# Seven up-projection pairs in seven products instead of five, and DRAM block sums handed out at other places: one core of a Trainium2

## The chip, the cores and the metric

The kernel runs on one core of one Trainium2 chip. The metric is the device time of one execution in microseconds: median 826.57 us of three runs before the change (824.71 to 828.17). Five engines work side by side: TensorE (PE; its weight loads, PEld, overlap its matmuls), VectorE (DVE), ScalarE (ACT), GpSimd (POOL) and SyncE (SP), which only issues DMAs. Sixteen DMA engines move data for the queues of SP, ACT and POOL.

## The reference, cut to what matters

One layer of an encoder, float32, 512 tokens of width 1024, 256 memory tokens:

```python
h = rmsnorm(x, pre_mix_g)
aq, ak, av, hq, hf_fwd, hf_bwd, hi, hg = split_columns(h @ w_in)
att = axial_gqa_attention(rope(rmsnorm(aq)), rope(rmsnorm(ak)), av)   # 8 heads of 64, 2 key heads
rec = hgrn2_group(hq, hf_fwd, hf_bwd, hi, hg)                         # 4 heads of 128, both directions
x = x + rmsnorm(concat(att, rec) @ w_out, post_mix_g)
x = x + rmsnorm(cross_attention(rmsnorm(x, pre_x_g), rmsnorm(mem), w_xq, w_xkv, w_xo), post_x_g)
u = rmsnorm(x, pre_ffn_g) @ w_up                                      # 1024 -> 2 x 2816
acc = conv_b + sum(shift(u, j - 1) * conv_w[j] for j in range(3))     # over positions
gate, val = split(acc)
x = x + rmsnorm((silu(gate) * val) @ w_down, post_ffn_g)              # 2816 -> 1024
```

## The kernel before, in words

**Every product in three matmuls.** TensorE multiplies in float32r. Each operand is split into a rounded high part and a low part (the rest), and a product is the sum of high x high, high x low and low x high (`mm3`, L242, its three matmuls on L243 to L245). The high part is a cast on ScalarE, the low part a subtraction on VectorE (`split`, L117, its two operations on L118 and L119).

**Weights come in units.** All projections but the last read weights in units of 128 x 1024, numbered in the order of their use: `plan` lists them, 0 to 65 (`N_MIX`) for the token mixing and the cross-attention, then the up projection, then 42 of the down projection. `take` and `unit` (L231 to L240) are called where TensorE wants the next unit; each call also hands out work for units `AHEAD` = 3 further on: `issue` (L198) loads the unit on SP's queue (`load_w`, L167), casts its high part and makes its low part. High and low parts have four buffers each (`wp`, L95), raw units two, and two more in the up projection (`raw_room`, L154). From unit 70 on loads also run ahead of the casts, `LOAD_AHEAD` = 5 units before their use (L228). For units 7 to 30 (`NEG_SCALAR`) the low part is not VectorE's: ScalarE writes minus the high part (L214) and a DMA on POOL's queue adds the raw weight from DRAM onto it (L217); for units 31 to 41 (`NEG_POOL`) POOL does the negation (L216).

**Order on the engines.** The framework sets the semaphores and lays the instructions of each engine in order, near the program's but not always in it; `tc.issue_after(ins)` holds an instruction behind another. Each engine works in order, and a wait at its head stops all behind it.

**Stages.** Input projection and four recurrent heads (`hgrn_core`), each a chain of small matmuls (L607) and VectorE products (L633); self-attention, woven with the keys and values of the memory; output projection and residual; queries and cross-attention; output projection and residual, where `turn_in` (L278) transposes the normalized rows into `hT`; up projection with convolution (`conv`, L1036); down projection.

The keys are transposed by `turn_k` (L711) into PSUM banks with the tag "b", two of them, which the memory's key projection uses as well. `rope_tables` (L668) scales the rope tables on ScalarE. The last `turn_in` also lets ScalarE copy the unsplit transposed rows to `fulls` (`keep`, L288 and L289).

**The up projection.** 22 pairs of a gate block and a value block of 128 columns. A whole pair takes two units and 2 x 8 products of 512 columns, three matmuls each. The pairs in `UP_S` = (5, 8, 11, 14, 17) are done by Strassen's scheme in Winograd's form (`strassen_pair`, L1094): seven products of 512 x 128 blocks with half of the tokens (256 columns) instead of eight. They take four units: "diag" and "side" are loaded, "sums" and "last" are sums of blocks that VectorE makes (`add_blocks`, L184). Differences of halves of the tokens come from `fulls` (`sum_of_h`, L1078, in pairs 2 and 3).

**The down projection.** The same scheme over the whole product: seven products (`PRODUCTS`) over the 22 activation blocks, in three groups (`GROUPS`). Four of the seven right sides are sums of blocks of `w_down`, built in DRAM by DMAs in six pieces each: a seed copy of one block and an accumulating DMA of another (`new_sums`, L989), called after pairs 2, 5, 8, 11, 14 and 17. The first seed of a kind goes to ACT's queue, seeds from an earlier sum to POOL's (L994), and the accumulating ones to POOL's (L998). The left sides are differences of activations (`group_sides`, L1001, called at pairs 18 and 19 and after the last) and are split by `left_side` (L1010), three ahead (`LAY_AHEAD`). For the (product, group) in `NEG_GROUP` their low part is a negation on POOL (L1023) and an accumulating DMA that reads the side itself (L1024). For product 3 the side is overwritten in place (L1014).

## Time and profile before

| | |
|---|---|
| time of the profiled execution | 825.72 us |
| its span, first to last instruction | 823.8 us |
| median of the three runs | 826.57 us |
| granted clock of TensorE | 0.999 |
| TensorE matmul / VectorE / ScalarE / GpSimd busy | 808.1 / 568.5 / 473.0 / 132.3 us |
| low parts by DMA on POOL's queue | 35 of 512 KB |
| DMAs for sums in DRAM (seeds and accumulating ones) | 48, of them 36 on POOL's queue and 12 on ACT's |
| moved by DMA | 135.66 MB, mean 165 GB/s |

How to read the rows: a row of the timeline has start (us), duration (us), engine, line, operation, output <- inputs, partitions x elements, how often in a row; in brackets stands how long the engine had stood idle before it, and what ended that. A row of groups has the count after the x, then busy us and mean ns. A row of waits has the engine and line that waited, what for, and us in total, times, longest. Matmuls overlap, so their step is read from starts, not from durations. A line in a helper (L118, L119, L243 to L245) stands for many uses; the tile's name tells them apart: `ps_b` is a PSUM bank of tag b, `wh` and `wl` are high and low parts of weights, `raw` and `tmp` unsplit weights, `sum_t` a sum in DRAM, `big` one of sixteen large buffers.

### The profile page before, as it was taken

Reading aid. Unit: us, or ns where it says so; the run is one execution under the profiler, and the core shown is the slowest. Engines: PE = TensorE matmul, PEld = TensorE weight load, DVE = VectorE, ACT = ScalarE, POOL = GpSimd, SP = SyncE. Lnnn points to the kernel's source line nnn. Section 1 sums busy time; section 2 is a strip of 40 time slices with the busy share of each in tenths; the row PEclk is TensorE's granted clock in tenths of the full one; section 3 lists DMA queues with packets and bytes.
Section 4 is the critical chain, followed back from the end, with each engine's and each line's share of the span. In section 5 each row is a group of like instructions: output and inputs, shape, how many; then the busy total and the mean of one; then the engine's idle time right before and its main releaser. Section 6 shows DMA issues by size and latency. Waiting matters only on the chain.

```text
span 823.8 us, 11495 instructions
## 1 busy us (share of the span) xinstructions
PE 808.1 (98%) x4354; PEld 690.6 (84%) x4354; DVE 568.5 (69%) x849; ACT 473.0 (57%) x785; POOL 132.3 (16%) x194
## 2 busy tenths in 40 slices
PE   9999999999999999999999999999999999999996
PEld 7878888889898887888888898889889888878884
DVE  5347486569886875855453769787687796868865
ACT  6666756369788874645543665444344453556651
POOL 0110211044233101300001300111110102100302
PEclk9999999999999999999999999999999999999999
DMA  9696753657668533252212145787898885368842
GB/s 316 186 283 134 173 112 95 129 140 162 160 155 191 116 136 120 77 179 78 88 43 101 37 163 153 205 232 202 224 279 217 232 250 146 103 200 295 249 124 102
DMA packets 39671, 135.66 MB, mean 165 GB/s; under 512 B 5120, under 2 KB 6656, under 8 KB 39424
## 3 DMA queue, kind: packets, MB, share of 16 engines
q1 hardware_dynamic: 25632, 86.03, 30.0%
q0 software_dynamic: 10960, 40.38, 25.5%
q10 hardware_dynamic: 3024, 8.53, 2.9%
q8 instruction: 34, 0.56, 0.3%
q14 instruction: 21, 0.17, 0.1%
HBM read 130.72 MB, written 25.17 MB: 189 GB/s over the span
## 4 chain that ended last, share of the span: by engine, by line
PE 84%; DMA 4%; DVE 4%; issue 3%; ACT 2%; POOL 2%; SPq 0%; POOLq 0%; DVEq 0%; ACTq 0%
PE ps_b L243 9%; PE ps_b L244 9%; PE ps_b L245 9%; PE ps_s L244 6%; PE ps_s L245 6%; PE ps_s L243 6%; PE ps_o L243 5%; PE ps_o L245 5%; PE ps_o L244 5%; PE ps_c L245 4%; PE ps_c L244 4%; PE ps_c L243 4%; PE ps_c L607 3%; PE ps_o L851 2%; PE ps_s L830 2%
## 5 line engine op out<-in xcount | busy, mean ns | idle before, releaser
L119 DVE TENSOR_TENSOR wl<-raw,wh 128x1024 fp32r<-128x1024 f32 (+1 forms) x75 | 90.7, 1212 | 64.1 <-ACT wh L118 63.8
L118 ACT CAST wh<-raw 128x1024 fp32r<-128x1024 f32 (+1 forms) x75 | 76.8, 1027 | 83.0 <-PE ps_b L244 25.7
L243 PE MATMUL ps_b<-big,wh 128*128 128x512 f32 (+1 forms) x340 | 122.4, 360 | 0.7 <-DVE big L119 0.7
L245 PE MATMUL ps_b<-big,wl 128*128 128x512 f32 (+1 forms) x340 | 120.5, 355 | 0.0
L244 PE MATMUL ps_b<-big,wh 128*128 128x512 f32 (+1 forms) x340 | 120.5, 354 | 0.0
L243 PEld LDWEIGHTS ps_b<-big,wh 128*128 128x128 f32 x340 | 64.3, 189 | 9.2 <-DVE big L119 0.9
L244 PEld LDWEIGHTS ps_b<-big,wh 128*128 128x128 f32 x340 | 64.3, 189 | 8.6
L245 PEld LDWEIGHTS ps_b<-big,wl 128*128 128x128 f32 x340 | 64.2, 189 | 8.7
L633 DVE TENSOR_TENSOR big<-big 128x512 f32<-128x512 f32 x64 | 48.4, 761 | 16.4 <-PE ps_c L607 10.1
L244 PE MATMUL ps_s<-wl,big 128*128 128x512 f32 (+1 forms) x140 | 53.4, 381 | 2.6 <-DVE wl L119 1.7
L243 PE MATMUL ps_s<-wh,big 128*128 128x512 f32 (+1 forms) x140 | 53.5, 384 | 0.4 <-DVE big L119 0.4
L245 PE MATMUL ps_s<-wh,big 128*128 128x512 f32 (+1 forms) x140 | 53.1, 379 | 0.0
L212 ACT CAST wh<-raw 128x1024 fp32r<-128x1024 f32 x35 | 36.8, 1052 | 26.7 <-PE ps_b L244 12.9
L217 POOL DMA_DIRECT2D wl<-in_w_dram x35 | 30.9, 883 | 120.1 <-ACT wl L214 105.1
L119 DVE TENSOR_TENSOR big<-ps_o,big 128x512 fp32r<-128x512 f32 x54 | 37.0, 688 | 14.1 <-ACT big L118 12.2
L998 POOL DMA_DIRECT2D sum_t<-in_wd_dram x24 | 19.7, 833 | 143.7 <-DMA sum_t<-in_wd_dram 86.8
L118 ACT CAST big<-ps_o 128x512 fp32r<-128x512 f32 x54 | 31.6, 589 | 17.2 <-PE ps_o L953 7.5
L243 PE MATMUL ps_o<-wh,big 128*128 128x512 f32 (+1 forms) x102 | 39.3, 386 | 0.0
L244 PE MATMUL ps_o<-wl,big 128*128 128x512 f32 (+1 forms) x102 | 38.2, 375 | 0.0
L245 PE MATMUL ps_o<-wh,big 128*128 128x512 f32 (+1 forms) x102 | 38.2, 374 | 0.0
L244 PE MATMUL ps_c<-big,wh 128*128 128x256 f32 (+1 forms) x112 | 37.6, 336 | 0.0
L243 PE MATMUL ps_c<-big,wh 128*128 128x256 f32 (+1 forms) x112 | 37.6, 336 | 0.0
(311 smaller groups left out, 2171.0 us busy)
## 6 DMA issues: line engine op xcount, KB each, us to landing
raw<-in_w_dram SPq DMA_DIRECT2D x85, 512.0 KB, 3.3
wl<-in_w_dram POOLq DMA_DIRECT2D x35, 512.0 KB, 5.4
sum_t<-in_wd_dram POOLq DMA_DIRECT2D x20, 512.0 KB, 8.1
tmp<-in_w_dram SPq DMA_DIRECT2D x14, 512.0 KB, 6.0
sum_t<-in_wd_dram ACTq DMA_DIRECT2D x10, 512.0 KB, 6.2
sum_t<-sum_t POOLq DMA_DIRECT2D x10, 512.0 KB, 5.2
big<-sum_t SPq DMA_DIRECT2D x10, 512.0 KB, 4.9
raw<-sum_t SPq DMA_DIRECT2D x10, 512.0 KB, 4.5
```

The source lines that it names most:

```text
L118: nc.scalar.copy(hi, src)
L119: (eng or nc.vector).tensor_sub(lo, src, hi.bitcast(F32))
L212: nc.scalar.copy(wh, raw)
L217: nc.gpsimd.dma_start(wl, io["w"][i], accum_op=ALU.add)
L243: nc.tensor.matmul(o, a[0], b[0], start=start, stop=False, skip_group_check=again)
L244: nc.tensor.matmul(o, a[0], b[1], start=False, stop=False, skip_group_check=again)
L245: last_mm[0] = nc.tensor.matmul(o, a[1], b[0], start=False, stop=stop, skip_group_check=again).ins
L607: nc.tensor.matmul(o[:, b, :], kc[:, blk(b)], pat(qk, b * P, [[2 * m, P // (2 * m)], [T + m, 2], [1, m]]), start=True, stop=True)
L633: nc.vector.tensor_tensor(out=c, in0=c, in1=pat(tt, toff + off, [[2, npair], [gap, 2], [0, m]]), op=ALU.mult)
L830: nc.tensor.matmul(s, qT[h // 4][:, h % 4, blk(qb)], kT[:, 2 * (h // 4) + c, :], start=c == 0, stop=c == 1)
L851: nc.tensor.matmul(o, vv[:, c, h // 4].rearrange("p a d -> p (a d)"), pt[j][:, c, :], start=c + j == 0, stop=c == 3 and j == 1)
L998: nc.gpsimd.dma_start(t, weight_block(second_name, width(u)), accum_op=ALU.add)
```

## The change

1. `UP_S` becomes (6, 8, 10, 12, 14, 16, 18): seven pairs in seven products instead of five, every second pair instead of every third. `group_sides` moves to pairs 19 and 20.
2. Low parts: "diag" units have their whole low part made by ScalarE's negation and POOL's accumulating DMA, "side" units the second half of it (`LOW_FROM`). Units 7 and 8 leave `NEG_SCALAR`.
3. Sums in DRAM: all 24 seeds are copies of blocks of `w_down` (no longer of sums) on SP's queue, one with each of the units 28 to 45 and 60 to 65, held behind that unit's load. The 24 adds stay on POOL's queue, one with each of the units 56 to 61 and, from pair 2 on, with units of whole pairs: both units of the pair, or only the first if the pair before is one in seven products. Ahead of each add POOL copies one column of that unit's low part, which makes it wait for it. Rows of the sums are padded by 32 elements. `new_sums` goes.
4. Loads of the up projection run seven units ahead instead of five.
5. `NEG_GROUP` loses (1, 1).
6. `turn_in` no longer copies to `fulls`; VectorE adds high and low parts into `fulls` in pair 2 (`full_h`), and all four `sum_of_h` are in pair 3.
7. `turn_k` takes banks with the tags "s", "s", "o", "o" for the four blocks.
8. The scaling of the rope tables is held behind the last gate of the recurrent heads so far; the sum of "diag" blocks is held behind VectorE's last low part.

The diff, cut to its core:

```diff
-UP_S = (5, 8, 11, 14, 17)
+UP_S = (6, 8, 10, 12, 14, 16, 18)
-SUMS = (("t1", "w11", "w12"), ("t3", "w22", "w12"), ("t2", "t1", "w22"), ("t4", "t2", "w21"))
+SUMS = (("t1", "w11", "w12"), ("t3", "w22", "w12"), ("t2", "w22", "t1"), ("t4", "w21", "t2"))
-LAY_AHEAD, LOAD_AHEAD = 3, 5
-SIDES_AT = (18, 19)
-NEG_GROUP = frozenset((p, 1) for p in (1, 2, 5, 6))
+LAY_AHEAD, LOAD_AHEAD = 3, (7, 5)
+SIDES_AT = (19, 20)
+LOW_FROM = {"diag": 0, "side": 512}
+SEEDS_AT = frozenset(range(28, 46)) | frozenset(range(60, 66))
+ADDS_AT = frozenset(range(56, 62))
+NEG_GROUP = frozenset((p, 1) for p in (2, 5, 6))
-NEG_SCALAR = frozenset(range(7, 31))
+NEG_SCALAR = frozenset(range(9, 31))
...
+            if i >= 2:
+                adds_at.update((len(plan), len(plan) + (i - 1 not in UP_S)))
             plan += [("w", whole), ("w", whole + 1)]
...
-            nc.vector.tensor_tensor(out=both..., in0=raw..., in1=mid..., op=ALU.add)
+            with tc.issue_after(last_low[0]):
+                nc.vector.tensor_tensor(out=both..., in0=raw..., in1=mid..., op=ALU.add)
...
-        if i in NEG_SCALAR or i in NEG_POOL:
-            nc.scalar.copy(wh, raw)
-            if i in NEG_SCALAR:
-                nc.scalar.mul(wl, wh.bitcast(F32), -1.0)
+        by_dma = 0 if i in NEG_SCALAR or i in NEG_POOL else LOW_FROM.get(kind, raw.shape[1])
+        nc.scalar.copy(wh, raw)
+        if by_dma:
+            last_low[0] = nc.vector.tensor_sub(wl[:, :by_dma], raw[:, :by_dma], wh[:, :by_dma].bitcast(F32)).ins
+        if by_dma < raw.shape[1]:
+            if i in NEG_POOL:
+                nc.gpsimd.tensor_scalar(wl, wh.bitcast(F32), -1.0, 0.0, op0=ALU.mult, op1=ALU.add)
             else:
-                nc.gpsimd.tensor_scalar(wl, wh.bitcast(F32), -1.0, 0.0, op0=ALU.mult, op1=ALU.add)
-            nc.gpsimd.dma_start(wl, io["w"][i], accum_op=ALU.add)
-        else:
-            split(wh, wl, raw)
-            add_blocks(kind, raw, raws[0] if raws else None)
+                nc.scalar.mul(wl[:, by_dma:], wh[:, by_dma:].bitcast(F32), -1.0)
+            nc.gpsimd.dma_start(wl[:, by_dma:], source(i)[:, by_dma:], accum_op=ALU.add)
+        add_blocks(kind, raw, raws[0] if raws else None)
         pending.append((wh, wl))
+        if i in SEEDS_AT:
+            seeds.popleft()()
+        if i in adds_at and adds:
+            with tc.issue_after(nc.gpsimd.tensor_copy(mark, wl[:, 0:1].bitcast(F32)).ins):
+                adds.popleft()()
...
+        def seed():
+            t = dram.tile([P, n + 32], F32, ...)[:, :n]
+            sums.setdefault(out_name, []).append(t)
+            with tc.issue_after(last_load[0]):
+                nc.sync.dma_start(t, weight_block(first_name, width(u)))
+        seeds.append(seed)
+        adds.append(lambda: nc.gpsimd.dma_start(sums[out_name][u], weight_block(second_name, width(u)),
+                                                accum_op=ALU.add))
+    for names in SUMS:
+        for u in range(6):
+            plan_sums(*names, u)
...
-        while N_MIX + 4 <= taken[0] and loaded[0] < min(N_UNITS, taken[0] + LOAD_AHEAD):
+        while N_MIX + 4 <= taken[0] and loaded[0] < min(N_UNITS, taken[0] + LOAD_AHEAD[loaded[0] >= N_DOWN]):
...
-            if keep:
-                nc.scalar.copy(keep[c][:, :, blk(b)], o)
...
-        for b in range(NB):
-            nc.scalar.mul(cs[:, :, b, :], cs[:, :, b, :], r[:, b:b + 1])
+        with tc.issue_after(last_gate[0]):
+            for b in range(NB):
+                nc.scalar.mul(cs[:, :, b, :], cs[:, :, b, :], r[:, b:b + 1])
...
-        o = bank("b").rearrange("p (k n) -> p k n", k=4)
+        o = bank(tm_tags[b]).rearrange("p (k n) -> p k n", k=4)
...
+    def full_h(k):
+        nc.vector.tensor_add(fulls[k], hT.hi[k].bitcast(F32), hT.lo[k].bitcast(F32))
...
-                if i < 4:
-                    sum_of_h(2 * i - 4 + c)
-        if i % 3 == 2 and i // 3 < 6:
-            new_sums(i // 3)
+                if i == 2:
+                    full_h(c)
+                elif i == 3:
+                    sum_of_h(2 * c)
+                    sum_of_h(2 * c + 1)
```

More of the change, by code (lines that the diff above doesn't have):

```diff
@@ L129, in layer @@
     pending, last_pow, last_mm = deque(), [None], [None]
-    issued, loaded, taken, last_load, rooms = [0], [0], [0], [None], [0]
+    issued, loaded, taken, last_load, last_low, rooms = [0], [0], [0], [None], [None], [0]
     sums, pair_sums = {}, {}
@@ L142, in layer @@
     plan = [("w", i) for i in range(N_MIX)]
-    whole = N_MIX
+    whole, adds_at = N_MIX, set(ADDS_AT)
     for i in range(NF):
@@ L165, in raw_room, with source @@
         return spare[0][:, k - 2, :]
+    def source(i):
+        kind, n = plan[i]
+        return io["w"][n] if kind == "w" else io["wu"][n, ("diag", "side").index(kind)]
     def load_w():
@@ L175, in load_w @@
         else:
-            kind, n = plan[i]
-            if kind in ("sums", "last"):
+            if plan[i][0] in ("sums", "last"):
                 return None
             raw = raw_room(i)
-            src = io["w"][n] if kind == "w" else io["wu"][n, ("diag", "side").index(kind)]
+            src = source(i)
         last_load[0] = nc.sync.dma_start(raw, src).ins
@@ L187, in add_blocks @@
             mid = ahead[:, :512]
-            nc.vector.tensor_tensor(out=both.rearrange("p (a n) -> p a n", a=2), in0=raw.rearrange("p (a n) -> p a n", a=2),
-                                    in1=mid[:, None, :].to_broadcast([P, 2, 512]), op=ALU.add)
+            with tc.issue_after(last_low[0]):
+                nc.vector.tensor_tensor(out=both.rearrange("p (a n) -> p a n", a=2),
+                                        in0=raw.rearrange("p (a n) -> p a n", a=2),
+                                        in1=mid[:, None, :].to_broadcast([P, 2, 512]), op=ALU.add)
             nc.vector.tensor_add(mid, both[:, :512], raw[:, half(1)])
@@ L276, in scale_rows, with turn_in @@
                                        op0=ALU.mult, op1=ALU.mult)
-    def turn_in(h, act, b, tags, keep=None):
+    def turn_in(h, act, b, tags):
         for c in range(2):
@@ L307, in residual_add, with between @@
                                        op0=ALU.mult, op1=ALU.add)
-    def between(x, g_post, g_pre, act, keep=None):
+    def between(x, g_post, g_pre, act):
         def first(b, y):
@@ L323, in second @@
                 scale_rows(x[b], ss[:, R:R + 1], g_pre, h, c)
-            return lambda: turn_in(h, act, b, y_tags[0][b] + y_tags[1][b], keep)
+            return lambda: turn_in(h, act, b, y_tags[0][b] + y_tags[1][b])
         return first, second
@@ L408, in layer @@
     nhalf = const.tile([P, 16], F32, name="nhalf")
+    mark = const.tile([P, 1], F32, name="mark")
     warm = tmp2()
@@ L533, in pair @@
         act.hi[i], act.lo[i] = t[:, 0], t[:, 1]
-    sg_box, heads, qkv, rec_done = [], {}, {}, [0]
+    sg_box, heads, qkv, rec_done, last_gate = [], {}, {}, [0], [None]
     def put_v(b, o):
@@ L569, in put @@
                 nc.scalar.activation(k, z, ACT.Sigmoid, scale=-1.0)
-                nc.scalar.activation(f, f, ACT.Identity, scale=oml[:, d, h:h + 1], bias=lb[:, d, h:h + 1])
+                last_gate[0] = nc.scalar.activation(f, f, ACT.Identity, scale=oml[:, d, h:h + 1],
+                                                    bias=lb[:, d, h:h + 1]).ins
                 nc.vector.scalar_tensor_tensor(out=qk[:, 0, 1 - d, :], in0=f, scalar=oml[:, d, h:h + 1], in1=q,
@@ L982, in layer @@
     hT = new_act()
-    fulls = [big([P, 4, T]) for _ in range(2)]
-    turns = res_second(ox, range(4), kv["x0"], between(x, g_post, g_pre, hT, fulls))
+    turns = res_second(ox, range(4), kv["x0"], between(x, g_post, g_pre, hT))
     acts, sides, gates, last_act = [], [], {}, [None]
     half_t = [slice(0, 256), slice(256, 512)]
-    def new_sums(u):
-        n = width(u).stop - width(u).start
-        for out_name, first_name, second_name in SUMS:
-            t = dram.tile([P, n], F32, name="sum_%s_%d" % (out_name, u), tag="sum_%s_%d" % (out_name, u))
-            if first_name in sums:
-                nc.gpsimd.dma_start(t, weight_block(first_name, width(u)))
-            else:
-                with tc.issue_after(last_act[0]):
-                    nc.scalar.dma_start(t, weight_block(first_name, width(u)))
-            nc.gpsimd.dma_start(t, weight_block(second_name, width(u)), accum_op=ALU.add)
-            sums.setdefault(out_name, []).append(t)
     def group_sides(g):
@@ L1071, in layer @@
                 turns.popleft()()
+    fulls = [big([P, 4, T]) for _ in range(2)]
     wide = [big([P, 2, 4, 256]) for _ in range(2)]
@@ L1134, in layer @@
                 conv(c, i, o)
-                if i < 4:
-                    sum_of_h(2 * i - 4 + c)
-        if i % 3 == 2 and i // 3 < 6:
-            new_sums(i // 3)
+                if i == 2:
[3 more added lines that the diff above has]
+                    sum_of_h(2 * c + 1)
+    assert not seeds and not adds
     def out_part(ss, y, i, cols, last, tag="ta"):
```

4 lines of the change are left out of this document (added).

## The prediction

> **What bounds the kernel now.** I read the page's head first, then the waits of the matmul engine, then the timeline around the longest of them.
>
> ```profile
> span 823.8 us, 11495 instructions
> ## 1 busy us (share of the span) xinstructions
> PE 808.1 (98%) x4354; PEld 690.6 (84%) x4354; DVE 568.5 (69%) x849; ACT 473.0 (57%) x785; POOL 132.3 (16%) x194
> ```
>
> TensorE is busy for 808.1 of 823.8 us. Nothing else comes near, so the time can fall in two ways only: fewer matmul columns, or fewer of the moments in which TensorE stands still. The view of waits names nearly all of those moments (us in total, times, longest).
>
> ```profile
> PE ps_s L244 <- DVE wl L119: 1.7, 1, 1.7
> PE ps_b L432 <- DVE tmp L413: 1.3, 1, 1.3
> PE ps_s L244 <- DMA wl<-in_w_dram: 1.0, 1, 1.0
> PE ps_b L243 <- DVE big L119: 0.7, 1, 0.7
> PE ps_b L715 <- ACT big L716: 0.7, 2, 0.5
> PE ps_o L243 <- ACT big L289: 0.6, 1, 0.6
> PE ps_c L607 <- DVE big L633: 0.6, 2, 0.4
> PE ps_c L282 <- ACT big L289: 0.5, 1, 0.5
> PE ps_s L243 <- DVE big L119: 0.4, 1, 0.4
> PE ps_c L607 <- DVE tmp L697: 0.4, 1, 0.4
> ```
>
> These ten add up to 7.9 us, and what follows them is 0.2 each. Rows 1, 3, 4, 5, 6 and 8 are what the edits called single waits aim at: 5.2 us. No list of waits can give more than that plus some weight reloads, so I expect a change of under 1.2%.
>
> **Two more pairs in seven products (term A).** Starts of matmul groups, from the timeline: a whole pair, the seven-product pair behind it, the whole pair after that.
>
> ```profile
> 517.07 0.39 PE L243 MATMUL ps_b<-big,wh 128*128 128x512 f32 x1
> ...
> 527.95 0.28 PE L243 MATMUL ps_c<-big,wh 128*128 128x256 f32 x1
> ...
> 538.01 0.40 PE L243 MATMUL ps_s<-big,wh 128*128 128x512 f32 x1
> ```
>
> A whole pair is 2 x 8 x 3 = 48 matmuls of 512 columns in 10.88 us; seven products are 7 x 4 x 3 = 84 of 256 columns in 10.06 us. One pair saves 0.82, two save 1.6 us. The column count alone would promise 12.5%, but a 256-column matmul steps at 0.120 us, more than half of 0.227. The Trainium skill (TensorE: Matmul & The Clock Gate, "Wait — 56ns, not 53.3ns?") gives a warm step of N / 2.4 GHz plus 2.5 ns, hence 0.216 and 0.109 us, by which two pairs would save 2.4 us. The trace's steps are longer in both sizes, so the trace decides.
>
> What hides the rest of such a pair is next. Its "diag" low parts, and half of "side", now come from ScalarE (a multiply by -1) and an accumulating DMA on POOL's queue instead of VectorE. Their costs:
>
> ```profile
> L212 ACT CAST wh<-raw 128x1024 fp32r<-128x1024 f32 x35 | 36.8, 1052 | 26.7 <-PE ps_b L244 12.9 <-PE ps_o L245 9.4 <-DMA raw<-in_w_dram 2.6
> ...
> L214 ACT ACTIVATE wl<-wh 128x1024 fp32r<-128x1024 f32 x24 | 25.4, 1057 | 0.2
> ...
> wl<-in_w_dram POOLq DMA_DIRECT2D x35, 512.0 KB, 5.4
> sum_t<-in_wd_dram POOLq DMA_DIRECT2D x20, 512.0 KB, 8.1
> ...
> DMA to landing us min/median/max: 5.1/6.7/10.4
> ```
>
> The last row is that of the low parts between 20 and 110 us. With four buffers, the cast of a diag waits for the unit four before it. Behind one whole pair that leaves the last product of the earlier pair (10.06 / 7 = 1.4 us) and a whole pair (10.88): 12.3 us. Cast 1.05 and multiply 1.06 leave 10.2 us for the DMA. The median of 5.4 fits with 4.8 us to spare, and 10.4 would be 0.2 late. I take nothing, as DMA is less loaded there than before (next part). By the fit in the Trainium skill (DMA: Bandwidth & Descriptors, "Anatomy of one DMA — SWDGE (gpsimd) path"; about 2.0 us plus the bytes at 436 GB/s), this DMA would take 3.2 us. The trace's fastest, 5.1 us, is already above it.
>
> **Sums handed out earlier.** Twenty-four seed copies leave ACT's and POOL's queues in the up projection. They go to SP's queue, 18 with the units of the attention stage and 6 in the cross output projection. Twenty-four adds go to POOL's queue, 6 with the queries' last units, 18 in the up projection, each behind a one-column copy that makes POOL wait for a weight's low part. Stages by windows (busy us of PE, PEld, DVE, ACT, POOL; clock; DMA share; GB/s):
>
> ```profile
> 189.00:218.00 29.00, 27.15 (x223) 26.16 (x222) 27.70 (x66) 24.02 (x44) 13.54 (x18) 1.00 0.85 200
> 217.00:330.00 113.00, 112.82 (x648) 95.75 (x648) 79.32 (x154) 84.87 (x180) 24.08 (x34) 1.00 0.53 138
> 480.00:711.00 231.00, 230.36 (x1271) 201.67 (x1270) 177.22 (x221) 110.95 (x138) 27.04 (x38) 1.00 0.73 203
> 495.30:517.07 21.77, 21.77 (x98) 18.01 (x97) 21.54 (x26) 11.76 (x15) 1.74 (x2) 1.00 0.59 163
> ...
> 442.21 0.22 POOL L268 TENSOR_SCALAR small<-small 128x1 f32<-128x1 f32 x1 [33.15 <-ACT tmp L299]
> ```
>
> In the up projection TensorE stands for 0.6 of 231 us, and that at its start (the L289 waits): the sums cost nothing where they are, and moving them earns nothing. What could it cost? The attention stage has DMA share to give: if 18 seeds of 512 KB move at the 203 GB/s of the third row they add 18 x 2.6 = 46 us of a share near 0.73 in 113 us, which brings 0.53 to about 0.83. Every weight there is asked for two units ahead, about 12 us (18 units in 113 us). SP has nothing to wait for at a seed, only the next weight behind it. POOL's adds at the queries stand ahead of the gain loads and of the row statistics, but POOL idles for 33.15 us before the first of those (the row at 442.21; its 0.22 us is also the price I put on a one-column copy). I take 0; if cover fails, a weight comes late by about one add, 8.1 us, once.
>
> **The wait at 731.6 (term E, 1.7).** Rows of VectorE:
>
> ```profile
> 728.36 1.23 DVE L1014 TENSOR_TENSOR big<-big 128x1024 f32<-128x1024 f32 x1 [4.83 <-DMA big<-big]
> 729.50 0.95 DVE L119 TENSOR_TENSOR big<-big 128x768 fp32r<-128x768 f32 x1
> 730.37 1.22 DVE L119 TENSOR_TENSOR wl<-raw,wh 128x1024 fp32r<-128x1024 f32 x1
> ```
>
> VectorE wants to overwrite a side of group 1, which the accumulating DMA for (product 1, group 1) is still reading. It stands for 4.83 us and the weight's low part behind it is late. With (1, 1) out of NEG_GROUP, ScalarE and VectorE make that low part: the wait goes and 1.22 us of VectorE comes in, so the low part (end 731.59) is ready 4.83 - 1.22 = 3.6 us earlier, at 728.0. TensorE wanted it 1.7 us before 731.6, at 729.9. The whole 1.7 us goes, with 1.9 to spare. (By the same row of 1.22 us for 1024 columns, VectorE is spared 1.2 us at each diag and 0.6 at each side.)
>
> **The DMA wait at 51.5 (term B, 1.0).** Units 7 and 8 no longer wait for POOL's DMA: VectorE, 69% busy overall, subtracts 1.2 us after the cast. Unit 9 is next with a DMA, a whole unit later. The whole 1.0 goes; at worst 0, if unit 9 then waits as long.
>
> **The second residual (term D, 0.6).** Eight extra copies by ScalarE (L289) go, and two additions by VectorE come in after the first up units. The bank that TensorE waits for is released by the copy and by the subtraction at 479.43:
>
> ```profile
> 478.29 1.22 DVE L119 TENSOR_TENSOR wl<-raw,wh 128x1024 fp32r<-128x1024 f32 x1
> 479.43 0.69 DVE L119 TENSOR_TENSOR big<-ps_o,big 128x512 fp32r<-128x512 f32 x1
> ...
> 480.79 0.39 PE L243 MATMUL ps_o<-big,wh 128*128 128x256 f32 x1 [0.64 <-ACT big L289]
> ```
>
> The subtraction ends at 480.12 whatever happens to the copy, and TensorE went on at 480.79. So the two L289 waits, 1.1 us in sum, give only the last 0.6; what is next is VectorE itself. If the weight's subtraction at 478.29 falls behind the other, it is 1.8; if another is put before it, 0. The additions: 2 x 2048 columns, by 1.23 for 1024 about 4.9 us, come to a stretch in which VectorE is 21.54 of 21.77 us busy (window from 495.30). It will run up to 5 us late there, against a lead of three units of 5.4 us less a cast and a subtraction, 14 us. I take 0.
>
> **Transposes of the keys (term C, 0.7).** With banks of their own, the two L715 waits and the L243 wait behind a "b" bank go: 1.4 us. But the window from 189 shows VectorE busy 27.70 of 29 us, and the head's chain through L633 goes through it; where TensorE comes earlier it may wait there. Between 0 and 1.8 (with the L697 row); I take half of 1.4. The rope scaling that is held back moves 1.3 us on ScalarE out of a stretch without a wait: 0.
>
> **Sum.** 1.6 + 1.7 + 1.0 + 0.6 + 0.7 = 5.6 us. The profiled execution took 825.72 us (span 823.8), the median of the three runs is 826.57. That gives 820.1 and 821.0; I say 820.5.
>
> **Rivals.** *VectorE keeps what TensorE gives up*: in the two stretches in which VectorE is full, C and D bring nothing and about 1 us more comes back in new short waits behind the added 4.9 us: 1.6 + 1.7 + 1.0 - 1.0 = 3.3, 822.4. For it: 27.70 of 29 and 21.54 of 21.77; against: the lead of three units. *Late diag low parts, the other side*: six of the seven pairs stand behind one whole pair only, and each such pair also hands out an add on POOL's queue. If the low part's DMA moves only after that add, it lands after up to 8.1 + 5.4 = 13.5 us, 3.3 over the 10.2: 6 x 3.3 = 19.8, 839.9. It decides from a landing of 10.2 on, eats the whole gain at 11.1, and makes the kernel slower by 0.5% at 11.8. Against it: the unit behind which the add stands is cast four products (5.7 us) before the diag, and the share of 0.73 falls as 24 seeds and 6 adds leave. *The change does not do what it says*: the order on each engine is laid by a scheduler, which put L1014 at 728 far ahead of its use; a new ill-placed instruction of that kind costs what the old one did, 1.7 to 4.8 us: about 824.
>
> **How the numbers follow.** Half a percent is 4.1 us, about what a measurement of this kernel can tell from no change; faster begins below 822.4. Forecast 0.58 (nearly all faster); VectorE 0.20 (0.08 faster, 0.12 not); late low parts 0.14 (0.08 up to the whole gain, 0.06 slower); ill-placed instruction 0.08, no change. Faster 0.64, same 0.30, slower 0.06. Range: below, all upper ends, 1.6 + 1.7 + 1.0 + 1.8 + 1.8 and 0.15 us of weight reload for each of eight waits, 9.1 from 825.72: 816.6. Above, 825.5 takes in the ill-placed instruction and late low parts near break-even.
>
> **What would show it.** Right: TensorE's matmul busy time falls by about 1.6 us or a little more, the rows 1, 3 and 6 of the waits are gone, and the up projection has no wait but its first. Wrong: a row "PE ... <- DMA wl<-in_wu_dram" six times over (late low parts), or waits for VectorE between 200 and 218 and 480 and 530 as long as the old ones. The prediction falls altogether if the seven-product pairs step slower than 10.06 us when only one whole pair lies between them.

## The result, and the profile after

| | before | changed |
|---|---|---|
| median, same chip | 826.14 us (824.71 to 828.17, the three runs of before and a fourth) | 819.34 us (818.57 to 819.99, 4 runs) |
| profiled execution | 825.72 us | 819.77 us |
| its span | 823.8 us | 817.7 us |

The ratio is 0.9916, 95% interval 0.9892 to 0.9939: 0.8% faster. The forecast was 820.5 us. The lines of the changed kernel are shifted: L243 to L245 are now L278 to L280, L118 and L119 are L121 and L122 (and L224 for the weights), L212 is L222, L214 is L229, L217 is L230, L607 is L642, L633 is L668, L715 is L751, L1014 is L1037. L236 is the one-column copy, L251 the add of a sum.

The head of the page and TensorE's waits after the change:

```profile
span 817.7 us, 11778 instructions
## 1 busy us (share of the span) xinstructions
PE 806.3 (99%) x4426; PEld 692.9 (85%) x4426; DVE 575.5 (70%) x867; ACT 480.4 (59%) x795; POOL 138.7 (17%) x216
```

```profile
PE ps_b L466 <- DVE tmp L447: 1.3, 1, 1.3
PE ps_c L642 <- DVE big L668: 0.6, 2, 0.4
PE ps_s L278 <- DVE tmp L1139: 0.6, 1, 0.6
PE ps_s L278 <- DVE big L122: 0.4, 1, 0.4
```

All six waits that the prediction took as aimed at are gone, and the L697 row with them. One row is new, the third: `tmp L1139`, at the first pair in seven products. TensorE's busy time fell by 1.8 us, the span by 6.1. So about 4.3 us came out of pauses, and more pairs cannot be the main part.

The order of a whole pair and a pair in seven products, from the timeline (starts of groups; 557.04 begins a pair in seven products, 567.11 a whole one, 578.02 the next in seven):

```profile
557.04 0.28 PE L278 MATMUL ps_s<-big,wh 128*128 128x256 f32 x1
...
567.11 0.40 PE L278 MATMUL ps_b<-big,wh 128*128 128x512 f32 x1
...
578.02 0.28 PE L278 MATMUL ps_c<-big,wh 128*128 128x256 f32 x1
```

10.07 and 10.91 us: the steps of before hold with one whole pair between. The low parts' DMAs and the stages by windows (columns as in the prediction):

```profile
wl<-in_w_dram POOLq DMA_DIRECT2D x33, 512.0 KB, 7.2
wl<-in_wu_dram POOLq DMA_DIRECT2D x7, 512.0 KB, 8.8
```

```profile
189.00:217.00 28.00, 27.87 (x232) 27.21 (x231) 26.44 (x65) 24.36 (x45) 13.54 (x18) 1.00 0.98 263
217.00:330.00 113.00, 112.82 (x644) 95.25 (x644) 81.00 (x157) 85.95 (x183) 24.20 (x34) 1.00 0.68 194
480.00:711.00 231.00, 230.45 (x1340) 204.64 (x1339) 185.51 (x238) 124.29 (x157) 33.54 (x52) 1.00 0.66 165
```

A low part lands in 8.8 us at the median, not 5.4. The seeds raised the DMA share of the attention stage from 0.53 to 0.68 (I had worked out 0.83), and no weight came late there. TensorE stands for 0.55 us of the up projection (0.64 before), but at another place:

```profile
540.11 1.22 DVE L224 TENSOR_TENSOR wl<-raw,wh 128x1024 fp32r<-128x1024 f32 x1
...
541.25 0.42 DVE L1139 TENSOR_TENSOR tmp<-ps_s,tmp 128x256 f32<-128x256 f32 x1
...
541.72 0.39 PE L278 MATMUL ps_s<-big,wh 128*128 128x256 f32 x1 [0.55 <-DVE tmp L1139]
```

VectorE must free the bank by L1139, a short subtraction, and that stands behind a weight's subtraction of 1.22 us.

Where the time went is read from TensorE's starts of the same matmuls in both traces (the lead is before minus after; a loss is negative):

| place (time before, us) | lead there | step |
|---|---|---|
| first weights, 8.4 | -0.6 | -0.6, start of the execution |
| after the wait at 51.5 | 0.5 | +1.1 (B) |
| 198 | 0.1 | -0.4, on the way |
| 418, after the keys' transposes | 2.0 | +1.9 (C) |
| 480.79, second residual | 3.5 | +1.5 (D) |
| 548.9, first pair in seven products | 2.8 | -0.7, the new wait |
| 709.1, end of the pairs | 4.35 | +1.6 (A) |
| 731.6 | 6.3 | +1.9 (E) |

The start isn't put down to the change: the kernels of the runs below are the same up to there, and at 9 us their executions stand from 0.1 us behind to 0.9 us ahead of the changed kernel's. What TensorE gains or loses in a run below is read behind the start.

### The profile page after: what moved, and what is told of

Its sections match the earlier page's. It is cut to its first block, busy times and chain, and to the rows that moved or that the text cites. A ratio compares the mean times of both kernels' runs of the same rounds, so it can differ in the third digit from the quotient of the medians.

```text
span 817.7 us, 11778 instructions
## 1 busy us (share of the span) xinstructions
PE 806.3 (99%) x4426; PEld 692.9 (85%) x4426; DVE 575.5 (70%) x867; ACT 480.4 (59%) x795; POOL 138.7 (17%) x216
## 4 chain that ended last, share of the span: by engine, by line
PE 95%; DVE 2%; ACT 1%; DMA 0%; POOL 0%; issue 0%; POOLq 0%; DVEq 0%; ACTq 0%
PE ps_b L279 10%; PE ps_b L280 10%; PE ps_b L278 10%; PE ps_s L280 7%; PE ps_s L278 7%; PE ps_s L279 7%; PE ps_o L278 5%; PE ps_o L280 5%; PE ps_o L279 5%; PE ps_c L280 5%; PE ps_c L278 5%; PE ps_c L279 5%; PE ps_c L642 3%; PE ps_o L887 2%; PE ps_s L866 2%; PE ps_o L876 2%
## 5 line engine op out<-in xcount | busy, mean ns | idle before, releaser
L222 ACT CAST wh<-raw 128x1024 fp32r<-128x1024 f32 x110 | 113.7, 1036 | 117.5 <-PE ps_b L279 36.2
L224 DVE TENSOR_TENSOR wl<-raw,wh 128x1024 fp32r<-128x1024 f32 (+1 forms) x77 | 92.3, 1200 | 72.1 <-ACT wh L222 72.0
L278 PE MATMUL ps_b<-big,wh 128*128 128x512 f32 (+1 forms) x344 | 122.7, 357 | 0.0
L280 PE MATMUL ps_b<-big,wl 128*128 128x512 f32 (+1 forms) x344 | 120.9, 351 | 0.0
L280 PEld LDWEIGHTS ps_b<-big,wl 128*128 128x128 f32 x344 | 65.0, 189 | 8.4
L278 PEld LDWEIGHTS ps_b<-big,wh 128*128 128x128 f32 x344 | 65.1, 189 | 8.1
L668 DVE TENSOR_TENSOR big<-big 128x512 f32<-128x512 f32 x64 | 48.1, 758 | 14.0 <-PE ps_c L642 6.5
L278 PE MATMUL ps_s<-wh,big 128*128 128x512 f32 (+1 forms) x140 | 53.2, 381 | 0.4 <-DVE big L122 0.4
L280 PE MATMUL ps_s<-wh,big 128*128 128x512 f32 (+1 forms) x140 | 53.0, 379 | 0.0
L230 POOL DMA_DIRECT2D wl<-in_w_dram x33 | 29.4, 891 | 121.6 <-ACT wl L229 86.6
L122 DVE TENSOR_TENSOR big<-ps_o,big 128x512 fp32r<-128x512 f32 x54 | 37.0, 687 | 14.1 <-ACT big L121 12.5
L121 ACT CAST big<-ps_o 128x512 fp32r<-128x512 f32 x54 | 31.7, 588 | 16.7 <-PE ps_o L989 7.5
L278 PE MATMUL ps_s<-big,wh 128*128 128x256 f32 (+1 forms) x120 | 40.1, 334 | 0.6 <-DVE tmp L1139 0.6
L222 ACT CAST wh<-tmp 128x1024 fp32r<-128x1024 f32 (+1 forms) x25 | 23.2, 928 | 28.5 <-PE ps_c L279 7.0
L279 PE MATMUL ps_s<-big,wh 128*128 128x256 f32 (+1 forms) x120 | 39.9, 333 | 0.0
L280 PE MATMUL ps_s<-big,wl 128*128 128x256 f32 (+1 forms) x120 | 39.9, 332 | 0.0
L278 PE MATMUL ps_o<-wh,big 128*128 128x512 f32 (+1 forms) x102 | 39.3, 385 | 0.0
L279 PE MATMUL ps_c<-big,wh 128*128 128x256 f32 (+1 forms) x120 | 39.1, 325 | 0.0
L278 PE MATMUL ps_c<-big,wh 128*128 128x256 f32 (+1 forms) x120 | 39.0, 325 | 0.0
```

The costliest lines, as they stand in the source:

```text
L121: nc.scalar.copy(hi, src)
L122: (eng or nc.vector).tensor_sub(lo, src, hi.bitcast(F32))
L222: nc.scalar.copy(wh, raw)
L224: last_low[0] = nc.vector.tensor_sub(wl[:, :by_dma], raw[:, :by_dma], wh[:, :by_dma].bitcast(F32)).ins
L230: nc.gpsimd.dma_start(wl[:, by_dma:], source(i)[:, by_dma:], accum_op=ALU.add)
L278: nc.tensor.matmul(o, a[0], b[0], start=start, stop=False, skip_group_check=again)
```

## The experiments

The medians of the kernel before on the chips of the runs below lie between 825.4 and 825.6 us. The first seven each undo one part of the changed kernel.

**Keys' transposes back in the "b" banks (C).**

```diff
-        o = bank(tm_tags[b]).rearrange("p (k n) -> p k n", k=4)
+        o = bank("b").rearrange("p (k n) -> p k n", k=4)
```

> The changed kernel with one edit undone: the four key transposes take banks of tag b again. Theory (the gain is a sum of separate waits, each standing where its own resource is): the waits at L751 and L278 between 205 and 217 us come back and TensorE is late by 1.9 us from there to the end (between the old and the changed kernel the lead grew by 1.9 us in that window), so about 821.2 us. Rival (that window is VectorE's, busy 26 to 28 us of 28, and the lead came from elsewhere, the DMA and queue relief): the waits come back for 0.7 us or less, below 820.0 us.

820.25 us, ratio 0.9939 (0.9925 to 0.9954). TensorE's waits, the rows that came back:

```profile
PE ps_b L278 <- DVE big L122: 0.7, 1, 0.7
PE ps_b L751 <- ACT big L752: 0.7, 2, 0.5
...
PE ps_c L642 <- DVE tmp L733: 0.4, 1, 0.4
```

1.8 us of waits: the three rows of before, to a tenth. VectorE is as full with the new banks (26.44 of 28 us in the window from 189) as it was (27.70 of 29), and still nothing waits for it instead. Only 0.8 us of this is left in the span (818.5 against 817.7): this execution's first weights are 0.8 us sooner, and the wait at 541.72, which a later TensorE doesn't meet, gives 0.4 back.

**(1, 1) back in the list of negated sides (E).**

```diff
-NEG_GROUP = frozenset((p, 1) for p in (2, 5, 6))
+NEG_GROUP = frozenset((p, 1) for p in (1, 2, 5, 6))
```

> The changed kernel with one edit undone: the low part of (product 1, group 1) is made by POOL's negation and an accumulating DMA again. Theory: VectorE stands behind that DMA before it overwrites the side, the weight behind it is late, TensorE waits once, 1.7 to 1.9 us between 720 and 730 us; about 821.2 us. Rival (the wait was there because the up projection's sums kept the DMA queues full, so the accumulating DMA was slow; with the sums gone from there it is now fast): the DMA lands 3 us sooner and the wait is below 0.5 us, 819.3 to 819.8 us.

819.0 us, 0.9925 (0.991 to 0.9941), and no wait between 725 and 731. My theory for this edit falls in this form; the rival's wait of under 0.5 us is what came. The timeline of ScalarE and GpSimd for that side:

```profile
710.16 1.04 ACT L1045 CAST big<-big 128x1024 fp32r<-128x1024 f32 x1
711.30 1.06 POOL L1046 TENSOR_SCALAR big<-big 128x1024 fp32r<-128x1024 f32 x1 [28.91 <-ACT big L1045]
712.66 0.90 POOL L1047 DMA_DIRECT2D big<-big  x1 [0.30 <-POOL big L1046]
```

Before, the cast began at 716.50 and the DMA was issued at 719.88; TensorE leads by 5.1 us there in this run, so that these stand for 711.4 and 714.8. The DMA now goes out 2.1 us sooner: the cast is 1.2 us sooner, and the negation takes 1.06 instead of 1.94 us. It also lands sooner after its issue, before and in this run:

```profile
big<-big POOLq DMA_DIRECT2D x1, 512.0 KB, 8.5
big<-big POOLq DMA_DIRECT2D x1, 512.0 KB, 4.8
```

So it lands 5.7 us sooner in all, and the side is free when VectorE overwrites it. Why it lands sooner, the sums that are gone or something else, no run separates. The run of the single waits below returns to this.

**Units 7 and 8 back to the DMA (B).**

```diff
-NEG_SCALAR = frozenset(range(9, 31))
+NEG_SCALAR = frozenset(range(7, 31))
```

> The changed kernel with one edit undone: the low parts of units 7 and 8 come by DMA on POOL's queue again. Theory: TensorE waits for unit 8's DMA near 51 us, 1.0 us; the core's chain behind it gives back 0.3 to 0.5 us, so 0.6 to 1.0 us at the end, 819.9 to 820.4 us. Rival (the wait was an accident of one execution, as its DMA took 8.4 us against a median of 5.4): no wait, 819.3 us.

819.83 us, 0.993 (0.9913 to 0.9946). The wait is back, at 52.58, and TensorE loses 1.5 us there against the changed kernel:

```profile
PE ps_s L279 <- DMA wl<-in_w_dram: 1.2, 1, 1.2
```

**The copies to `fulls` back, no additions (D).** `turn_in` copies again, `full_h` is not called, the `sum_of_h` are in pairs 2 and 3.

> The changed kernel with one edit undone: ScalarE copies the unsplit rows to fulls again, VectorE's two additions go, and the four sums of h are spread over pairs 2 and 3 as before. Theory: the two L289-like waits at 476 to 480 us come back and cost 1.5 us, and the new wait at 541.7 us (VectorE late behind the two additions, 0.7 us) goes: 0.8 us slower in all, 820.1 us. Rival 1 (the copies cost what the subtraction left over, 0.6 us, as predicted): 819.2 us. Rival 2 (the wait at 541.7 us has nothing to do with the additions, it is the order in the first seven-product pair): it stays, 820.8 us.

820.36 us, 0.9936 (0.9921 to 0.9952):

```profile
PE ps_o L278 <- ACT big L324: 0.6, 1, 0.6
...
PE ps_c L317 <- ACT big L324: 0.5, 1, 0.5
```

TensorE loses 1.4 us at this place against the changed kernel (0.15 ahead at 467, 1.2 behind at 477), a little more than both waits, and gains 0.7 back at 541.72, where the new wait is gone. So that wait belongs to the two additions, or to the differences of halves, which move with them; the edit as a whole is worth 0.7 us.

**Five pairs in seven products, all else as changed (A).**

```diff
-UP_S = (6, 8, 10, 12, 14, 16, 18)
+UP_S = (6, 8, 10, 12, 14)
```

> The changed kernel with five seven-product pairs (6, 8, 10, 12, 14) instead of seven, all else as changed. Theory: each pair saves 10.88 - 10.06 = 0.82 us, so two fewer cost 1.6 us: 820.9 us, and no wait appears or goes. Rival (a dense row of such pairs costs TensorE something of its own, steps or bank changes that no wait names): the two are worth 1 us or less, 820.3 us or below.

821.0 us, 0.9945 (0.993 to 0.996); the span is 1.5 us longer, at the two places where the pairs are missing and nowhere else. 0.75 us a pair beside the predicted 0.82.

**The sums at their old places and on their old queues.** Seeds and adds again by `new_sums`, after pairs 2, 5, 8, 11, 14 and 17; low parts of the seven pairs by DMA as in the changed kernel.

```diff
-SEEDS_AT = frozenset(range(28, 46)) | frozenset(range(60, 66))
+SEEDS_AT = frozenset()
...
+        if i % 3 == 2 and i // 3 < 6:
+            new_sums(i // 3)
```

> The changed kernel with the sums in DRAM built as before: seeds on ACT's and POOL's queues, seed and add by turns after pairs 2, 5, 8, 11, 14, 17; seven pairs, low parts by DMA and all else as changed. Theory (the sums cost nothing where they were, and the low parts' DMA has 10.2 us of which it uses 8.8): POOL's queue now holds a seed or add that waits for the one before it (4 to 6 us each) ahead of the diag's DMA, so the low parts come late in some pairs, 0 to 3 us each; with no such wait 819.3 us, at most 835. That is, moving the sums earns nothing by itself but makes room on POOL's queue for the low parts. Rival (the sums' place matters to neither): 819.3 us and no DMA wait.

856.64 us, 1.0376 (1.0349 to 1.0403). This is the largest effect of the study; the prediction had put it at nothing, and the expectation at 835 us at most. TensorE's waits, then ScalarE's and GpSimd's timeline at the first of them (L229 makes a "diag" unit's negative, L1026 and L1030 are seed and add, L230 the low part's DMA):

```profile
PE ps_o L277 <- DMA wl<-in_wu_dram: 10.5, 2, 9.8
PE ps_c L277 <- DMA wl<-in_wu_dram: 10.3, 2, 9.3
PE ps_b L277 <- DMA wl<-in_wu_dram: 9.7, 2, 7.1
```

```profile
520.38 1.05 ACT L229 ACTIVATE wl<-wh 128x1024 fp32r<-128x1024 f32 x1
...
520.61 0.82 POOL L1030 DMA_DIRECT2D sum_t<-in_wd_dram  x1 [5.24 <-DMA sum_t<-sum_t]
...
527.81 0.52 POOL L1026 DMA_DIRECT2D sum_t<-sum_t  x1 [6.39 <-DMA sum_t<-in_wd_dram]
...
532.45 0.81 POOL L1030 DMA_DIRECT2D sum_t<-in_wd_dram  x1 [4.12 <-DMA sum_t<-sum_t]
533.05 2.02 POOL L230 DMA_DIRECT2D wl<-in_wu_dram  x2
```

The negative is ready at 521.43, and its DMA is issued at 533.05, 11.6 us later. GpSimd stands before a seed until the earlier add has landed, and before an add until its seed has; the low part's issue is behind both. At this pair the DMA itself is slower too, 9.5 us to its landing instead of 5.3; over all low parts of the pairs it isn't, 7.8 us at the median in both traces between 500 and 700 (720 in this run). The waits add up to 30.5 us. TensorE's busy time is 7.2 us longer as well (813.5 against 806.3); the last section shows what a pause does to it.

**All low parts of the pairs by VectorE, sums as changed.**

```diff
-LOW_FROM = {"diag": 0, "side": 512}
+LOW_FROM = {}
```

> The changed kernel with the low parts of diag and side made by VectorE as in the old kernel; POOL's queue then holds only the adds in the up projection. Theory (VectorE has room: 185 of 231 us are busy in the up projection, 7 x 1.8 = 13 us more make 198): TensorE waits at most in the first such pair, 0.7 us as now and up to 1 us more; 819.3 to 820.3 us. Rival (every second pair in seven products fills VectorE for its stretch: 17.0 busy of 21.6 us plus 1.8 is 18.8, and its low parts and bank reads then come late in each): 0.5 us or more in each of six pairs, above 822 us.

822.1 us (820.19 to 823.27), 0.9951 (0.9934 to 0.9968). One wait grows:

```profile
PE ps_s L278 <- DVE tmp L1139: 1.7, 1, 1.7
```

It is the wait at 541.72, 0.6 in the changed kernel; no other is added. The profile is of a run of 820.32 us. The median is 1.8 us above it and above the range that I gave, and what the three slower runs (822.1 to 823.3) lost, no profile shows; of the rival's six waits the one profile has none. In the profiled one VectorE has room for all seven pairs' low parts, but not in the stretch into which the two additions fall.

**Pairs beside each other.**

```diff
-UP_S = (6, 8, 10, 12, 14, 16, 18)
+UP_S = (6, 7, 9, 10, 12, 13, 15)
```

> The changed kernel with its seven pairs side by side where possible: (6, 7, 9, 10, 12, 13, 15). A diag directly behind another such pair has four products and the last one, 5.8 + 1.4 = 7.2 us, from the free buffer to its use, and needs cast 1.05, multiply 1.06 and a DMA of 8.8 us (the median in the changed kernel), 10.9 in all. Theory (the rival of late low parts decides by the lead alone): pairs 7, 10 and 13 wait for their DMA, about 3.7 us each, 11 us in all: 830 us. Rival (the DMA only takes 8.8 us because nothing asks for it sooner): it lands in 5.4 us, the three waits are below 0.4 us each, 819.3 to 820.5 us.

824.36 us (10 runs), 0.9984 (0.9967 to 1.0). Three pairs follow another one directly, and at each of the three TensorE waits:

```profile
PE ps_o L280 <- DMA wl<-in_wu_dram: 3.1, 3, 1.1
```

About 1.0 us each instead of the 3.7 worked out. That the low part's DMA is what TensorE waits for is shown; its price was wrong. The landing at pair 10:

```profile
wl<-in_wu_dram POOLq DMA_DIRECT2D x1, 512.0 KB, 6.2
```

At pairs 7, 10 and 13 it takes 7.1, 6.2 and 6.1 us, not 8.8. From the free buffer (571.63 at pair 10) to where TensorE stands (579.21) there are 7.6 us, near my 7.2. So the rival was half right: the DMA is faster here, but not by enough. At these three pairs no add stands ahead of it on GpSimd's queue for 13 us or more; in the changed kernel one stands 5.3 us ahead of the "diag" DMA of every pair but the first, and it takes 7.7 to 9.3 us. At the first pair the add stands 4.0 us ahead and the DMA still takes 5.3, so the add alone isn't the reason; what is stays open. The waits are 3.1 of the 4.3 us by which this kernel's span is longer.

**An eighth pair, and the additions ahead of pair 2.**

```diff
-UP_S = (6, 8, 10, 12, 14, 16, 18)
+UP_S = (6, 8, 10, 12, 14, 16, 18, 20)
...
+    for k in range(2):
+        full_h(k)
     for i in range(2, NF):
```

With them two more adds are handed out early (units 54 and 55), and the second `group_sides` moves to pair 21.

> The changed kernel with both additions into fulls placed ahead of pair 2 and the differences of halves in pairs 2 and 3, and with an eighth pair in seven products (6 to 20, every second one). Theory (VectorE's late additions are what TensorE waits for at 541.7 us, and a pair in seven products costs 10.06 us against 10.88 wherever one whole pair lies between): the wait of 0.55 us at 541.72 goes, the last pairs end 0.8 us sooner, 819.3 - 0.6 - 0.8 = 817.9 us. Rival (VectorE or the low parts by DMA have no room for another pair): the eighth pair brings a wait of 0.5 us or more at its sums or at the sides of the down projection, 818.7 us or above.

824.96 us (12 runs), 0.9989 (0.9977 to 1.0001). The rival, in another form than I gave it: VectorE's wait at the first pair is gone, and a late low part stands there, once.

```profile
PE ps_b L280 <- DMA wl<-in_wu_dram: 4.4, 1, 4.4
```

```profile
524.41 1.65 POOL L236 COPY mark<-wl 128x1 f32<-128x1 f32 x1 [2.93 <-DVE wl L224]
...
525.27 1.07 ACT L229 ACTIVATE wl<-wh 128x1024 fp32r<-128x1024 f32 x1
...
526.00 0.81 POOL L251 DMA_DIRECT2D sum_t<-sum_t  x1
526.63 1.09 POOL L230 DMA_DIRECT2D wl<-in_wu_dram  x1
```

Here GpSimd doesn't stand: the low part's DMA is issued at once after its negative, but 0.6 us behind an add, which a one-column copy of 1.65 us had delayed. It lands after 12.7 us (the longest of this stage; 9.3 in the changed kernel), 3.8 us behind the add. That is the rival of the late diag low parts, for which I had worked out 13.5 us. In the changed kernel the add ahead of that pair goes out 4.0 us before the low part, and TensorE doesn't wait. The pause costs more than its 4.4 us; the last section shows it. The rival comes in its own form as well: the eighth pair gives about 0.8 us up to the end of the pairs, and behind it, where VectorE makes the sides of the down projection, TensorE waits 0.5 us for a weight's low part and 0.3 for a side and loses 1.4. This run has three edits, and which of them brought the add beside the low part it can't tell.

**The kernel before with the single waits' edits alone.** Banks, (1, 1), units 7 and 8, and the copies to `fulls` replaced by two additions ahead of pair 2. Five pairs, their low parts by VectorE, and the sums as before.

> The kernel before with only the four edits aimed at single waits: own banks for the keys' transposes, (1, 1) out of NEG_GROUP, units 7 and 8 out of NEG_SCALAR, no copies to fulls in the second residual but two additions ahead of pair 2. Five pairs and the sums stay as before. Theory (each edit takes its own waits, and the landmarks of the change hold without the pairs and the sums): 1.9 us between 198 and 219, 1.9 at 731, 1.1 at 51.5, 1.5 at 480, 6.4 in all, 0.8 of it given back at the start: 819 to 820.5 us. Rival (the wait at 731 went because the sums left the stage of the pairs, since putting (1, 1) back into the changed kernel brought no wait): with the sums in their old places a wait of 1 us or more stays between 725 and 735, 821.5 us or above.

819.5 us (818.77 to 823.47, 6 runs), 0.9941 (0.9919 to 0.9963): as fast as the changed kernel within the intervals, and its span is 817.0 us. Its head and the longest of its waits; none of the six is left:

```profile
span 817.0 us, 11481 instructions
...
PE 806.6 (99%) x4354; PEld 689.9 (84%) x4354; DVE 573.9 (70%) x854; ACT 466.6 (57%) x775; POOL 127.5 (16%) x190
```

```profile
PE ps_b L430 <- DVE tmp L411: 1.3, 1, 1.3
```

Against the kernel before, TensorE gains 1.1 us at 51.5, 2.1 between 198 and 234, 1.4 at the second residual and 1.8 at 731, 6.4 in all. Two things follow. The waits' edits carry the whole gain; two more pairs, the moved sums and the low parts by DMA together add nothing that these times can tell. And taking (1, 1) out does remove the wait at 731 by itself, with the sums at their old places; the second experiment shows that the rest of the change removes it too. Either is enough.

**The adds in fours at the old places, seeds early.** The adds are issued four at a time after pairs 2, 5, 8, 11, 14 and 17 in the program, without the one-column copy.

> The changed kernel with the seeds early as it has them, but all 24 adds in fours after pairs 2, 5, 8, 11, 14 and 17, with no one-column copy ahead of them. Theory A (the 30 us of waits with the old sums came from GpSimd standing at the head of its queue for a seed or an earlier add to land, with the low parts' DMAs behind it): no add waits for a seed here, GpSimd issues four in about 3 us, low parts come 3 us later at most on the queue, TensorE waits for them 0 to 3 us in all: 819 to 823 us. Theory B (the bytes of the adds queued ahead hold up the low parts): a low part behind four adds lands 8 to 20 us late, and with three or more pairs behind such a four TensorE waits 15 us or more: 834 us or above.

836.46 us, 1.0133 (1.0114 to 1.0152), by neither theory. The trace shows why: nothing holds the adds back, and the scheduler laid all 24 between 186 and 461 us, close behind their seeds. GpSimd's waits, and the attention stage:

```profile
POOL sum_t L248 <- DMA sum_t<-in_wd_dram: 142.7, 17, 44.4
```

```profile
217.00:330.00 113.00, 102.34 (x600) 86.78 (x599) 75.49 (x147) 80.78 (x166) 34.03 (x38) 0.97 1.00 256
```

GpSimd stands for seeds for 142.7 us between 186 and 461 us. In the attention stage the DMA engines are full (1.00), and TensorE loses 10.7 of 113 us. In the up projection TensorE waits for nothing. So this run doesn't decide between a queue that stands and bytes that hold up; it shows what the one-column copy is for: it ties an add to a weight that is made late.

**Seven pairs, the sums at their old places, no low part by DMA.** The kernel of the sums' run with `LOW_FROM = {}` and the additions ahead of pair 2.

> The changed kernel with its seven pairs in seven products and its waits' edits, but with the sums in DRAM built at their old places and on their old queues, all low parts of the pairs in seven products by VectorE (no DMA for them), and the two additions into fulls ahead of pair 2. Theory (the sums cost nothing at their old places as long as no low part's DMA stands behind them on GpSimd's queue, and VectorE has room for the low parts of seven pairs): the kernel before with the waits' edits alone took 819.5 us, two more pairs take 1.6 us off: 817.9 us. Rival (with two more pairs VectorE has no room: without the DMAs for low parts the changed kernel waited 1.7 us for VectorE's copy at the first pair; or the last sums come late for the down projection): 819.5 us or above, with waits of 1.5 us or more for VectorE or for a sum's DMA.

818.27 us (817.96 to 818.47, 5 runs), 0.9911 (0.989 to 0.9932). Its head and the up projection:

```profile
span 816.3 us, 11665 instructions
...
PE 805.4 (99%) x4426; PEld 692.7 (85%) x4426; DVE 584.9 (72%) x874; ACT 468.8 (57%) x781; POOL 126.2 (15%) x190
```

```profile
480.00:711.00 231.00, 231.00 (x1342) 205.24 (x1341) 196.12 (x247) 113.90 (x143) 26.98 (x38) 1.00 0.74 204
```

TensorE doesn't stand once in the up projection, and VectorE, with all low parts, is busy for 196 of 231 us. Against the kernel with the waits' edits alone the two more pairs gain 1.65 us between 544 and 704. Against the changed kernel this one leads by 0.3 us from the first weights, by 1.2 from 541.72 on and by 1.3 from 670 on. So 0.8 of the 1.0 us is the wait at 541.72, which goes with the additions' place; the low parts and the sums make 0.2. It is the fastest of the study; the intervals of its ratio and of the changed kernel's overlap, so that it beats the changed kernel is shown by the traces (by 1.0 us) and not by the times.

## Why the prediction came out as it did

The total fell where it was forecast, and for its main reason: waits that are named in the profile were removed and little came in their place. That it fell so near is in part luck: C and D brought 2.1 us more than forecast, and 1.7 us that were in no term went the other way. One sign of being right failed, as the up projection has a wait that isn't at its start. By steps, predicted and measured:

| step | predicted, us | measured, us |
|---|---|---|
| A, two more pairs | 1.6 | 1.6; 1.5 undone; 1.65 in the kernel with old sums |
| B, DMA wait at 51.5 | 1.0 | 1.1; 1.5 where undone |
| C, keys' transposes | 0.7 | 1.9; waits of 1.8 where undone |
| D, second residual | 0.6 | 1.5; 1.4 where undone |
| E, wait at 731.6 | 1.7 | 1.9; 1.8 by the edit alone |
| VectorE's additions | 0 | -0.7 at 541.72 |
| start of the execution and the rest | 0 | -1.0 |

**A.** Right, and the reason too: the step of the trace held. By the rule of the Trainium skill that the prediction weighed (TensorE: Matmul & The Clock Gate, "Wait — 56ns, not 53.3ns?") the two pairs would have given 2.4; the three measurements lie at the trace's 1.6.

**B.** Right. It took only the first place: the next unit with a DMA, unit 9, brings no wait.

**C.** The mechanism was right, the term too small. I halved 1.4 because VectorE was busy for 27.70 of 29 us. A busy share says nothing of which engine is late at the wait in question: the undone edit brings back exactly the rows of before, and the L697 row, which I had left to the upper end, belongs to them. The upper end, 1.8, was the measurement.

**D.** The step that failed is that "the subtraction ends at 480.12 whatever happens to the copy". Both L289 waits went, and the subtraction itself (now at 476.43) runs 3.0 us sooner while TensorE led by 2.1 up to there. The copies of the earlier blocks stand in the same queue of ScalarE's. Its timeline before the change:

```profile
460.30 0.57 ACT L289 COPY big<-ps_b 128x512 f32<-128x512 f32 x1
...
463.54 0.59 ACT L289 COPY big<-ps_s 128x512 f32<-128x512 f32 x1 [2.18 <-DVE big L119]
...
464.61 1.05 ACT L118 CAST wh<-raw 128x1024 fp32r<-128x1024 f32 x1
```

ScalarE stood 2.18 us before the second copy, with a weight's cast behind it; that cast is at 462.05 now. I followed the last copy and took the chain that feeds it as given. No run takes the earlier copies out alone, so that the 0.9 us over my 0.6 come through this queue is read from the timelines and not tested. Against it stands the price of the additions, which I set to 0 from a lead of 14 us. That lead is the weights'; L1139 frees a PSUM bank and has none. VectorE runs without a pause from 498.8 to 536 us, with the additions in it (2.29 us each, at 502 and 507), and the first bank in seven products that it must free pays 0.55 us and a weight reload. With the additions ahead of pair 2 no such wait is seen. The 0.15 us of weight reload per wait, for which the prediction gave no row, is about right where it can be read: the wait of 1.66 us at 731.6 was worth 1.8.

**E.** The size was right, and the edit does it alone. The chain I gave, a DMA that lands late, is not tied to this edit: with (1, 1) left in, a DMA that is issued 2.1 us sooner and lands in 4.8 instead of 8.5 us does as well.

**The sums.** "Moving them earns nothing" is right and incomplete. At their old places they cost nothing as long as no low part's DMA shares GpSimd's queue: the last kernel has them there and doesn't wait. With low parts by DMA they cost 37 us. The two edits belong together, and I priced one with the old state of the other. What the pair of edits was to relieve, VectorE, had room: against the last kernel they gained nothing (0.2 us behind it, too little to tell; the other 0.8 us is the additions').

**The late low parts.** I took a landing of 5.4 us from the row for other units and had 4.8 us to spare; the landing is 8.8 at the median, and what was left is about 1.4. The mechanism of the rival is real: in the run with eight pairs one low part behind an add took 12.7 us, and TensorE stood. In the run with the old sums, too, three "diag" low parts issued 0.5 to 0.6 us behind a seed or an add landed 3.5 to 4.3 us behind it. In the changed kernel the slowest took 9.3 us, 0.9 under the 10.2.

**VectorE keeps what TensorE gives up.** In the keys' stage nothing of it is seen; in the up projection it took 0.7 us, the rival's 1 us in the place that it named.

## What to carry to other kernels

Price an edit in the state that the other edits leave behind: here a DMA put on a queue made 48 harmless DMAs of another edit cost 37 us, and running the parts in separate groups showed that the waits' edits carry the gain and the rest gives little more than it costs. A full engine beside a wait is no reason to halve the wait's worth; ask which instruction frees the thing that is waited for, and what it stands behind. A queue in order passes on every wait at its head, so an issue that must be in time should share it only with issues that never wait.

## What the runs showed of the hardware

**A pause costs TensorE its clock.** In the run with eight pairs, behind the pause of 4.38 us (window, columns as above):

```profile
539.40:544.20 4.80, 4.80 (x22) 4.80 (x23) 0.00 (x0) 0.37 (x1) 0.00 (x0) 0.50 0.12 35
```

The granted clock is 0.50 for these 4.8 us (and already from 2.4 us into the pause on, in the window 537.40 to 539.38), and matmuls of 256 columns step at 0.213 instead of 0.120 us; 22 of them cost about 2.1 us more. So the pause is worth 6.5 us, most of why that kernel's span is 6.1 us longer than the changed one's. The three pauses of 1.0 us in the run with pairs side by side left the clock at 1.00, and so did one of 2.07 us in the run with the adds in fours. Behind a pause of 2.58 us in the run with the old sums (641.10 to 643.68) it is at half again:

```profile
645.20:648.40 3.20, 3.20 (x17) 3.20 (x16) 0.00 (x0) 1.31 (x2) 0.84 (x1) 0.50 0.37 67
```

The Trainium skill (TensorE: Matmul & The Clock Gate, "What's actually happening") says that the clock drops to half after an idle window of about 3.4 us and comes back after about as long a busy one. The pauses of 4.38, 2.07 and 1.0 us agree with that; the one of 2.58 us doesn't, so here a shorter pause was enough. The half clock of 4.8 us lasted somewhat longer than the page's 3.4.

**A copy of one column can take 2.18 us.** I had priced it at 0.22; 24 of them have a median of 0.185. The long one, beside two of VectorE's differences of halves in the changed kernel:

```profile
519.11 2.35 DVE L1107 TENSOR_TENSOR big<-big 128x1024 f32<-128x1024 f32 x2
519.32 2.18 POOL L236 COPY mark<-wl 128x1 f32<-128x1 f32 x1 [7.60 <-DVE wl L224]
```

It ends with them, within 0.04 us. The Trainium skill (SBUF — State Buffer, "Who interferes with whom") states that a VectorE instruction with two inputs in SBUF contends with a GpSimd instruction that reads SBUF; this row agrees. So does the negation of (1, 1): before, from 717.64 on, it took 1.94 us beside two subtractions of VectorE's, the second of which (512 columns) took 1.53 instead of 0.68; in the second experiment it took 1.06, and VectorE's subtraction beside it (768 columns, from 711.37 on) took 1.79 us instead of 0.95. So either of the two can be the one that is slowed. The copy delayed an add here, and nothing waited for that; in the run with eight pairs the copy of 1.65 us put an add beside a low part.

**Accumulating DMAs of low parts on GpSimd's queue** landed in 5.3 to 9.3 us in the changed kernel's up projection, with a median of 7.8 over both sizes (256 and 512 KB), in 6.1 to 7.1 for the three of 512 KB with no add close ahead (pairs beside each other), and in 12.7 behind an add issued 0.6 us earlier.
